# A two-layer hybrid encoder on one core: queries rotated beside their products, the rotary key on 128 partitions at the layer's front, latents left unscaled

## The chip, the core and the metric

The kernel runs on one core of a Trainium2 chip. A core has TensorE (matrix products into PSUM), VectorE, ScalarE and GpSimd for elementwise work, SyncE, which issues most DMA transfers, and DMA engines. Each engine works through its own list of instructions in order; they meet only at semaphores. The metric is the device time of one execution in microseconds (us). Before the change the median of three executions was 1465.46 us (1462.36 to 1467.71).

## The reference

The model is an encoder of two layers over 1024 tokens of width 1024, all in fp32. Per layer, cut to what matters here:

```
u = rmsnorm(h, ln_mix) @ w_in            # split by columns:
c_q, c_kv, k_rope, gate_a, gq, gk, gv, lr_f, lr_b, gate_g = split(u)
# attention (4 heads): latents normed, expanded; a shared rotary key
q = rmsnorm(c_q, q_norm) @ w_uq          # per head 128 plain + 64 rotary columns
k, v = rmsnorm(c_kv, kv_norm) @ w_ukv
scores = q_plain @ k.T + rope(q_rot) @ rope(k_rope).T
y_mla = softmax(scores * scale) @ v * silu(gate_a)
# gated linear attention (4 heads), forward and backward
la = log_sigmoid(lr @ w_g + b_g) / 16    # decay, cumulated in chunks of 64
y_gla = rmsnorm(gla(gq, gk, gv, la)) * silu(gate_g)
h = h + concat(y_mla, y_gla) @ w_out
h = h + sigmoid(rmsnorm(h) @ w_gate) * (p[i] @ w_proj)
```

`rope(x)` splits 64 columns into halves x1, x2 and gives (x1 cos - x2 sin, x1 sin + x2 cos). `rmsnorm(x)` is x / sqrt(mean(x²) + 1e-6), times a gain.

## The kernel before

Everything is kept transposed: 128 features on the partitions, 1024 tokens along the free dimension. To reach fp32 accuracy every operand is split into a high and a low part (names end in h and l), and each product is three matmuls: high·high, low·high, high·low (`mm3`, L165). A tile of the input projection (`in_tile`, L314) is 48 matmuls of 512 columns; its weights come in two halves through `load_split` (L139): a DMA into wr, a ScalarE copy that makes wh (L146), a ScalarE copy with scale -1 that puts -wh into wl (L150) and a GpSimd DMA that adds the weights to it (L151). There are five buffers each of wh and wl, so a split waits until TensorE is through with the block five loads earlier that has the buffer. PSUM has tiles of two banks under two tags, "mm" and "aux", two tiles each.

The input's norm factor r_x (1 / rms per token, as a full tile) is computed by `rstd` (L174): ScalarE makes sqh, VectorE sql, TensorE sums over the partitions (L185), VectorE does a Newton iteration on small tiles (nwa, nwy, nwt). Since the norm is not applied to the projection's input, each evacuation multiplies by r_x.

A layer is a list of steps, written as a string per layer (ORDER, L50). Q, K, V, G: queries, keys, values and gates of the linear attention. Z: decay of one head (z, Exp, Ln, scans on VectorE, d, exponentials). S: chunk states of one head (transposes L420, products L433, ten ScalarE copies, 28 VectorE state steps L460, then the masked products `afb`, L472). O: output of one head and its norm (o, o2, sqh). C and D: the key-value and query latents (`latent_tile`, L507: the VectorE product craw, then Square on ScalarE); N and M: their norms (L514). A: attention gates. X: the two tiles of rotary query columns of all heads (`q_pairs`), which stay in both "aux" tiles of PSUM, and the loads of the cosine and sine tables. E: the rotated key (`rotary_key`, L583), on 32 partitions at a time. T: the rotated queries (`rotary_queries`, L607), whose parts go to the heads' tiles qs by 16 DMAs. H: a head's plain queries (qh, ql). k, v: a head's keys (kh, kll) and values. s: scores, b: attention products, y and w: output projection. A "+" swaps the PSUM tag of a step.

The string gives priorities. A scheduler then sets the order of each engine's list from them and from its own estimate of times, so that a step moved in the string can move others.

Of the kernel before, what the change touches and what calls it, by code (L numbers as in the profile page):

```python
# [19 lines left out]
P = 128  # L20
# [26 lines left out]


WTAG = "aux"
ORDER = ("K0 R0 Q0 G0+ Z0 V0 K1 S0 Z1 V1 O0 S1 Q1 D0 Z2 G1 G2 P0 O1 S2 C0 Z3 D1 C1 N0 D2 O2 S3 G3 M0 A0 O3 X0 A1 E0 A2 A3+ H0 k0 T0 s0 v0 H2 k1+ s1 k2 b0 H1 k3 s2 y1 b1 H3+ s3 b2 v1 s4 y0 y3 b3 y2 s5 b4 w0 w1+ s6 w2 b5 w3+ s7 w4 b6 w5+ s8 w6 w7 b7",  # L50
         "Q0 K0 Z0 V0 S0 Z1 V1 S1 Q1 K1 Z2 G0 O0 S2 G1 Z3 G2+ C0 O1 D0 O2 S3 G3 C1 N0 D1 D2+ O3 M0 X0 A0 A1 E0 A2 k0 y2 H0 A3 T0 s0 v0 H3 k1+ s1 H1 b0 H2 s2 k2 b1 s3 y0 k3+ b2 v1 s4 y3 y1 b3 s5 b4 w0 w1+ s6 w2+ b5 w3 s7 w4 b6 w5+ s8 w6+ w7 b7")

ENG = dict(at="V", qi="V", qb="P", og="P", gate="P", sq="V", kT="A", put="A", o="A", ple="A", hadd="V")
TCKW = {"schedule_with_timeline_sim": True}
# [3 lines left out]
def hybrid_encoder(ctx: ExitStack, tc: tile.TileContext, xT, pT, pos, vecs, w_in, wq, wk, wv,  # L58
# [112 lines left out]
                    nc.tensor.matmul(ps[:, c, :], lhsT=a, rhs=b[:, c * HC:(c + 1) * HC],  # L171
                                     start=(i == 0 and j == 0), stop=(i == n - 1 and j == 2))

    def rstd(acc, width, n=S, tmp=st, res=mt, col=None):  # L174

        if isinstance(acc, tuple):
            mat, parts = ones_r.bitcast(F32), acc
        else:
            mat, parts = ones_r, (tmp(dt=F32R, name="sqh"), tmp(dt=F32R, name="sql"))
            split(parts[0][:, :n], parts[1][:, :n], acc)  # L180
        ps = flat(bank2("aux"))
        for c in range(0, n, HC):
# [39 lines left out]
    h1d = dram([8, P, S], "h1d")  # L222
    cosd = dram([32, S], "cosd")
    sind = dram([32, S], "sind")

    def ple_projection(i):
        ops = []
# [12 lines left out]
        for g in range(4):  # L240
            hi, lo = load_split(w_proj[i, g], HC)
            for c in range(2):
# [49 lines left out]
    for L in range(DEPTH):  # L292
# [213 lines left out]

        def latent_tile(t, s2, tile=mt):  # L507
            ps = in_tile(t)
            o = tile(name="craw")
            nc.vector.tensor_tensor(o, flat(ps), r_x, op=ALU.mult)  # L510
            s2.add(o)
            return o

        def latent_norm(raws, s2, off, width):  # L514
            r = rstd(s2.acc, width)
            res = []
            for j, raw in enumerate(raws):
                nc.vector.scalar_tensor_tensor(raw, raw, gv(off, j), r, op0=ALU.mult, op1=ALU.mult)
# [63 lines left out]

        def rotary_key():  # L583

            cos, sin = xx[2:]
            t1, t2 = mt(name="t1"), mt(name="t2")
            k1, k2 = slice(64, 96), slice(96, 128)
            nc.vector.tensor_tensor(t1[0:32], small[k1], cos[k1], op=ALU.mult)
            nc.vector.tensor_tensor(t2[0:32], small[k2], sin[k2], op=ALU.mult)
            nc.vector.tensor_tensor(t1[32:64], small[k1], sin[k1], op=ALU.mult)  # L590
            nc.vector.tensor_tensor(t2[32:64], small[k2], cos[k2], op=ALU.mult)
            nc.vector.tensor_tensor(t1[0:32], t1[0:32], t2[0:32], op=ALU.subtract)
            nc.vector.tensor_tensor(t1[32:64], t1[32:64], t2[32:64], op=ALU.add)
# [353 lines left out]
```

## Time and profile before

| what | before |
|---|---|
| median of three executions | 1465.46 us |
| the profiled execution | 1466.21 us, span 1464.5 us |
| TensorE busy | 1377.6 us, 94% |
| VectorE, ScalarE, GpSimd busy | 856.5, 721.3, 427.6 us |
| granted TensorE clock, mean | 0.979 of full speed |
| DMA | 163.93 MB, 112 GB/s over the span |

The span is what the profiled execution's trace covers; the rest of its time lies around it. Busy times of VectorE and ScalarE are far from the span, so their sums alone say little: what counts is where TensorE stands idle and which engine's instruction ends that. In a timeline's row the bracket at the end gives the idle time before the instruction and what released it. The first layer runs to about 760 us, the second to the end.

### The profile page before, as it was taken

What the parts mean: (1) busy time and instruction counts of PE and PEld (TensorE: products, weight loads), DVE (VectorE), ACT (ScalarE), POOL (GpSimd) and SP (SyncE); (2) the same over time, 40 slices, a digit from 0 to 9 for tenths busy, and PEclk for the clock granted to TensorE, in tenths of its full rate; (3) what the DMA queues carried; (4) which work ended last, traced back from release to release, by engine and by line L of the source; (5) the groups of instructions that cost most, each with busy time, mean ns of one, the idle gap of its engine ahead of it and who ended that gap; (6) DMA issues with size and microseconds to landing.
All of it is one profiled execution on the core that took longest, in us unless ns stands there. A gap on an engine that the chain in (4) does not pass through costs nothing. (4 is left out here: it accounts for less than half of the span.)

```text
span 1464.5 us, 21076 instructions
## 1 busy us (share of the span) xinstructions
PE 1377.6 (94%) x8400; PEld 1167.1 (80%) x8400; DVE 856.5 (58%) x1196; ACT 721.3 (49%) x1013; POOL 427.6 (29%) x312
## 2 busy tenths in 40 slices
PE   8999899998999999999999999889989999999984
PEld 6799778876778788888889877778767888878984
DVE  2576745788446544464455686667745564455547
ACT  6565475544355443364545555534444453345531
POOL 4321212122346454112432211212145564311210
PEclk9999999999999999999999999999999999999997
DMA  8653545346431223355765343324651213335853
GB/s 288 178 124 76 112 104 170 82 101 145 126 82 43 71 67 94 67 112 152 208 155 121 73 95 79 87 66 96 177 134 47 65 51 80 102 73 112 210 130 123
DMA packets 77793, 163.93 MB, mean 112 GB/s; under 512 B 9536, under 2 KB 17088, under 8 KB 77696
## 3 DMA queue, kind: packets, MB, share of 16 engines
q1 hardware_dynamic: 51200, 116.19, 25.9%
q0 software_dynamic: 26496, 46.41, 18.9%
q8 instruction: 66, 1.08, 0.3%
q14 instruction: 31, 0.25, 0.1%
HBM read 128.74 MB, written 25.43 MB: 105 GB/s over the span
## 5 line engine op out<-in xcount | busy, mean ns | idle before, releaser
L150 ACT ACTIVATE wl<-wr 128x512 fp32r<-128x512 f32 (+2 forms) x176 | 107.4, 610 | 316.8 <-PE ps L171 287.5
L680 POOL TENSOR_SCALAR sc<-sc,sums 128x1024 f32<-128x1024 f32 x64 | 182.1, 2856 | 101.5 <-DVE sums L679 95.3
L151 POOL DMA_DIRECT2D wl<-in_w_in x84 | 72.5, 877 | 353.1 <-ACT wl L150 314.8
L146 ACT ACTIVATE wh<-wr 128x512 fp32r<-128x512 f32 (+2 forms) x184 | 110.8, 603 | 30.3 <-PE ps L171 11.9
L678 ACT ACTIVATE sc<-ps,top 128x1024 f32<-128x1024 f32 x64 | 71.4, 1116 | 72.8 <-DVE top L677 67.8
L677 DVE TENSOR_REDUCE top<-ps 128x1 f32<-128x1024 f32 x64 | 78.3, 1224 | 44.2 <-PE ps L672 44.1
L171 PE MATMUL ps<-xh,wh 128*128 128x512 f32 x288 | 92.3, 400 | 10.1 <-DVE gate L366 4.6
L133 DVE TENSOR_TENSOR el<-ps,eh 128x1024 fp32r<-128x1024 f32 x64 | 78.1, 1220 | 40.4 <-ACT eh L132 40.2
L171 PE MATMUL ps<-x0h,wh 128*128 128x512 f32 x288 | 91.5, 399 | 8.9 <-DVE t L613 5.0
L460 DVE SCALAR_TENSOR_TENSOR s<-s,last 64x128 f32<-64x128 f32 x208 | 77.0, 370 | 36.8 <-ACT s L102 29.8
L171 PE MATMUL ps<-x0h,wl 128*128 128x512 f32 x288 | 91.4, 397 | 0.8 <-DMA wl<-in_w_in 0.8
L171 PE MATMUL ps<-xh,wl 128*128 128x512 f32 x288 | 91.5, 396 | 0.0
L171 PE MATMUL ps<-xl,wh 128*128 128x512 f32 x288 | 90.8, 395 | 0.0
L171 PE MATMUL ps<-x0l,wh 128*128 128x512 f32 x288 | 90.4, 395 | 0.0
L132 ACT ACTIVATE eh<-ps 128x1024 fp32r<-128x1024 f32 x64 | 65.4, 1022 | 38.9 <-PE ps L693 38.9
L171 PE MATMUL ps<-yh,wh 128*128 128x512 f32 x256 | 79.8, 393 | 1.2 <-DVE h L732 0.9
L171 PE MATMUL ps<-yl,wh 128*128 128x512 f32 x256 | 79.5, 391 | 0.0
L171 PE MATMUL ps<-yh,wl 128*128 128x512 f32 x256 | 79.5, 390 | 0.0
L151 POOL DMA_DIRECT2D wl<-in_w_out x32 | 27.9, 873 | 175.0 <-ACT wl L150 174.9
L171 PEld LDWEIGHTS ps<-xh,wh 128*128 128x128 f32 x288 | 54.4, 192 | 22.8 <-DVE gate L366 5.0
L693 PE MATMUL ps<-ident,sc 128*128 128x128 f32 x512 | 66.3, 273 | 6.2 <-DVE ql L130 3.1
L171 PEld LDWEIGHTS ps<-x0h,wh 128*128 128x128 f32 x288 | 54.7, 192 | 21.6 <-DVE t L613 5.7
(257 smaller groups left out, 3569.0 us busy)
## 6 DMA issues: line engine op xcount, KB each, us to landing
wr<-in_w_in SPq DMA_DIRECT2D x88, 256.0 KB, 3.4
wl<-in_w_in POOLq DMA_DIRECT2D x84, 256.0 KB, 4.9
wr<-in_w_gate SPq DMA_DIRECT2D x40, 256.0 KB, 3.2
projd<-po SPq DMA_DIRECT2D x16, 512.0 KB, 4.6
wr<-in_w_out SPq DMA_DIRECT2D x32, 256.0 KB, 3.3
wl<-in_w_out POOLq DMA_DIRECT2D x32, 256.0 KB, 4.7
wl<-in_w_gate POOLq DMA_DIRECT2D x32, 256.0 KB, 4.7
xraw<-in_xT SPq DMA_DIRECT2D x8, 512.0 KB, 5.9
```

The lines of the kernel that those rows point to most:

```text
L132: nc.scalar.activation(hi, src, AF.Copy)
L133: nc.vector.tensor_tensor(lo, src, hi.bitcast(F32), op=ALU.subtract)
L146: nc.scalar.activation(hi[:, :n], raw[:, :n], AF.Copy)
L150: nc.scalar.activation(lo[:, :n], raw[:, :n], AF.Copy, scale=-1.0)
L151: nc.gpsimd.dma_start(lo[:, :n], src, accum_op=ALU.add)
L171: nc.tensor.matmul(ps[:, c, :], lhsT=a, rhs=b[:, c * HC:(c + 1) * HC], start=(i == 0 and j == 0), stop=(i == n - 1 and j == 2))
L460: nc.vector.scalar_tensor_tensor(state(n)[rows], state(m)[rows], alpha[rows, m:m + 1], state(n)[rows], op0=ALU.mult, op1=ALU.add)
L677: nc.vector.tensor_reduce(m, flat(ps), axis=AX.X, op=ALU.max, negate=True)
L678: nc.scalar.activation(e, flat(ps), AF.Exp, bias=m, accum_out=sums[:, b:b + 1])
L680: nc.gpsimd.tensor_scalar(e, e, sums[:, b:b + 1], None, op0=ALU.mult)
L693: nc.tensor.transpose(out=ps[:, j, b * P:(b + 1) * P], in_=e[:, kt], identity=ident)
```

## The change

Three parts. The order strings: E goes from behind A1 (beside X0) to the layer's front, and T goes from behind H0, k0 (first layer) or A3 (second) to right behind X0. The key: `rotary_key` fetches its two halves by eight DMAs into 128 partitions (four token quarters of 32 features), does its products 256 columns wide there, splits once, writes the parts to a DRAM tile krd and loads ks and kl from it; sine and cosine stay in a constant tile sc4 for this. The latents: `latent_tile` copies the PSUM tile unscaled with ScalarE, Square reads PSUM too, and `latent_norm` corrects the epsilon term: since craw lacks the factor r_x, the norm needs EPS times (mean(x²) + EPS) in place of EPS, which `ax` and `base` carry.

```diff
@@ ORDER
-  "K0 R0 Q0 G0+ Z0 V0 ... O3 X0 A1 E0 A2 A3+ H0 k0 T0 s0 v0 ..."
+  "K0 R0 E0 Q0 G0+ Z0 V0 ... O3 X0 T0 A1 A2 A3+ H0 k0 s0 v0 ..."
-  "Q0 K0 Z0 V0 ... X0 A0 A1 E0 A2 k0 y2 H0 A3 T0 s0 v0 ..."
+  "Q0 K0 E0 Z0 V0 ... X0 T0 A0 A1 A2 k0 y2 H0 A3 s0 v0 ..."
@@ rstd
-        nc.vector.tensor_scalar(a, ..., 0.5 / width, 0.5 * EPS,
-                                op0=ALU.mult, op1=ALU.add)
+        nc.vector.tensor_scalar(a, ..., 0.5 / width,
+                                0.0 if base is not None else 0.5 * EPS, op0=ALU.mult, op1=ALU.add)
+        if base is not None:
+            nc.vector.scalar_tensor_tensor(a, base, EPS, a, op0=ALU.mult, op1=ALU.add)
+        if ax is not None:
+            nc.vector.tensor_copy(ax, a)
@@ latent_tile
             o = tile(name="craw")
-            nc.vector.tensor_tensor(o, flat(ps), r_x, op=ALU.mult)
-            s2.add(o)
+            nc.scalar.activation(o, flat(ps), AF.Copy)
+            s2.add(flat(ps))
@@ latent_norm
-            r = rstd(s2.acc, width)
+            r = rstd(s2.acc, width, base=ax)
@@ rotary_key
-            cos, sin = xx[2:]
-            t1, t2 = mt(name="t1"), mt(name="t2")
...
-            nc.scalar.activation(ks[0:64], t1[0:64], AF.Copy)
-            nc.scalar.activation(ks[64:128], t1[0:64], AF.Copy)
-            for half in (slice(0, 64), slice(64, 128)):
-                nc.vector.tensor_tensor(kl[half], t1[0:64], ks[0:64].bitcast(F32), op=ALU.subtract)
+            n = S // 4
+            work = mt(name="kr")
+            k1, k2, u1, u2 = (work[:, i * n:(i + 1) * n] for i in range(4))
+            rot = mt(name="krot")[:, :2 * n]
+            cos, sin = sc4[:, 0], sc4[:, 1]
+            for b in range(4):
+                for k, row in ((k1, 64), (k2, 96)):
+                    nc.sync.dma_start(k[b * 32:(b + 1) * 32], small[row:row + 32, b * n:(b + 1) * n])
+            for x1, x2, o, op in ((cos, sin, rot[:, :n], ALU.subtract), (sin, cos, rot[:, n:], ALU.add)):
+                nc.vector.tensor_tensor(u1, k1, x1, op=ALU.mult)
+                nc.vector.tensor_tensor(u2, k2, x2, op=ALU.mult)
+                nc.vector.tensor_tensor(o, u1, u2, op=op)
+            parts = mt(F32R, "krp").rearrange("p (h c) -> p h c", h=2)
+            split(parts[:, 0], parts[:, 1], rot)
             ks, kl = mt(F32R, "ks"), mt(F32R, "kl")
+            for i, t in enumerate((ks, kl)):
+                for b in range(4):
+                    nc.sync.dma_start(krd[L, i, :, :, b * n:(b + 1) * n].rearrange("j f n -> f j n"),
+                                      parts[b * 32:(b + 1) * 32, i].bitcast(F32).rearrange("p (j n) -> p j n", j=2))
+                for half in (slice(0, 64), slice(64, 128)):
+                    nc.sync.dma_start(t[half].bitcast(F32), krd[L, i].rearrange("j f n -> (j f) n"))
```

Lines of the changed file stand 10 to 20 higher than before: L393 to L396 there are L382 to L385 here (z, a, and its two functions), L633 to L635 are L613 to L615, L377 is L366, L697 is L677, L514 is L503, L210 is L205.

ScalarE at the front of the second layer, before. z_6460 is the bias step of Z0, wl and wh with 6658 belong to V0's fourth weight block, those with 6858, 6913, 6968 and 7023 to V1's four.

```order
L150 ACTIVATE wl_6658<-wr_6656 128x512
L146 ACTIVATE wh_6657<-wr_6656 128x512
L150 ACTIVATE wl_6858<-wr_6856 128x512
L146 ACTIVATE wh_6857<-wr_6856 128x512
L382 ACTIVATE z_6460<-ps_6457,vec_92 128x1024
L383 ACTIVATE a_6461<-ps_6457,vec_92 128x1024
```

The same place of the changed kernel: z_6520 is Z0's bias step, krp_6500 the key's split, 6973, 7028 and 7083 are V1's second to fourth blocks.

```order
L150 ACTIVATE wl_6973<-wr_6971 128x512
L146 ACTIVATE wh_6972<-wr_6971 128x512
L132 ACTIVATE krp_6500<-krot_6485 128x512
L150 ACTIVATE wl_7028<-wr_7026 128x512
L146 ACTIVATE wh_7027<-wr_7026 128x512
L150 ACTIVATE wl_7083<-wr_7081 128x512
L146 ACTIVATE wh_7082<-wr_7081 128x512
L393 ACTIVATE z_6520<-ps_6517,vec_92 128x1024
L394 ACTIVATE a_6521<-ps_6517,vec_92 128x1024
```

Z0's steps moved behind the key's split and the splits of three more weight blocks.

ScalarE at Z1 of the second layer, before (s1_6727 is the last of the ten state copies, 7197 is the second block of Q1).

```order
L102 ACTIVATE s1_6727<-ps_6744 64x128
L382 ACTIVATE z_6825<-ps_6822,vec_92 128x1024
L383 ACTIVATE a_6826<-ps_6822,vec_92 128x1024
L384 ACTIVATE a_6826<-a_6826 128x1024
L385 ACT_TABLE_LOAD
L385 ACTIVATE a_6826<-a_6826 128x1024
L150 ACTIVATE wl_7197<-wr_7195 128x512
```

And in the changed kernel (7319 and 7326 are K1's two blocks).

```order
L102 ACTIVATE s1_6787<-ps_6804 64x128
L150 ACTIVATE wl_7319<-wr_7317 128x512
L146 ACTIVATE wh_7318<-wr_7317 128x512
L393 ACTIVATE z_6885<-ps_6882,vec_92 128x1024
L394 ACTIVATE a_6886<-ps_6882,vec_92 128x1024
L395 ACTIVATE a_6886<-a_6886 128x1024
L150 ACTIVATE wl_7326<-wr_7324 128x512
L146 ACTIVATE wh_7325<-wr_7324 128x512
L396 ACT_TABLE_LOAD
L396 ACTIVATE a_6886<-a_6886 128x1024
```

A weight block's split now stands between Z1's Exp and its Ln.

VectorE at the rotated queries of the first layer, before (ps_3082 and ps_3108 are X0's two tiles in PSUM, gate_3348 the gate of A3).

```order
L130 SCALAR_TENSOR_TENSOR ql_3379<-ps_3359,qh_3378 128x1024
L503 SCALAR_TENSOR_TENSOR o_3041<-o_3041,vec_92,rstd_3054 128x1024
L133 TENSOR_TENSOR kll_3403<-ps_3389,kh_3402 128x1024
L613 TENSOR_TENSOR t1_3406<-ps_3082,cos_3127 128x1024
L614 TENSOR_TENSOR t2_3407<-ps_3108,sin_3128 128x1024
L615 TENSOR_TENSOR t1_3406<-t1_3406,t2_3407 128x1024
L130 SCALAR_TENSOR_TENSOR rl_3412<-t1_3406,rh_3411 128x1024
L613 TENSOR_TENSOR t1_3415<-ps_3082,sin_3128 128x1024
L614 TENSOR_TENSOR t2_3416<-ps_3108,cos_3127 128x1024
L615 TENSOR_TENSOR t1_3415<-t1_3415,t2_3416 128x1024
L130 SCALAR_TENSOR_TENSOR rl_3421<-t1_3415,rh_3420 128x1024
L366 TENSOR_TENSOR gate_3348<-ps_3285,rstd_351 128x1024
```

And in the changed kernel (ps_3121 and ps_3147 are X0's tiles; ahead of the first row here stand t1_3176 from ps_3121 and the gate of A2).

```order
L210 STREAM_TRANSPOSE rstd_3093<-nwy_3096 128x1024
L634 TENSOR_TENSOR t2_3177<-ps_3147,sin_3167 128x1024
L514 SCALAR_TENSOR_TENSOR o_3080<-o_3080,vec_92,rstd_3093 128x1024
L635 TENSOR_TENSOR t1_3176<-t1_3176,t2_3177 128x1024
L130 SCALAR_TENSOR_TENSOR rl_3182<-t1_3176,rh_3181 128x1024
L633 TENSOR_TENSOR t1_3185<-ps_3121,sin_3167 128x1024
L634 TENSOR_TENSOR t2_3186<-ps_3147,cos_3166 128x1024
L635 TENSOR_TENSOR t1_3185<-t1_3185,t2_3186 128x1024
L130 SCALAR_TENSOR_TENSOR rl_3191<-t1_3185,rh_3190 128x1024
L377 TENSOR_TENSOR gate_3411<-ps_3348,rstd_354 128x1024
L130 SCALAR_TENSOR_TENSOR ql_3442<-ps_3422,qh_3441 128x1024
L133 TENSOR_TENSOR kll_3466<-ps_3452,kh_3465 128x1024
```

The queries' rotation moved ahead of ql and kll, and the gate of A3 with it.

## Rows read from the trace of the kernel before

**Rows 1.** The page: busy us of an engine, share, instructions

```profile
PE 1377.6 (94%) x8400; PEld 1167.1 (80%) x8400; DVE 856.5 (58%) x1196; ACT 721.3 (49%) x1013; POOL 427.6 (29%) x312
```

**Rows 2.** Timeline of TensorE, first layer: start us, us, instruction, [idle before]

```profile
350.20 0.61 PE L171 MATMUL ps<-ch,wh 128*128 128x512 f32 x2
...
369.63 1.22 PE L171 MATMUL ps<-x0h,wh 128*128 128x512 f32 x2 [4.99 <-DVE t L613]
...
374.75 0.62 PE L171 MATMUL ps<-x0l,wh 128*128 128x512 f32 x2
...
382.00 0.39 PE L672 MATMUL ps<-kh,qh 128*128 128x512 f32 x1
```

**Rows 3.** Windows: start:end us, length, busy times, granted clock, DMA

```profile
370.00:383.00 13.00, 13.00 (x53) 10.58 (x53) 3.96 (x4) 2.87 (x5) 1.30 (x2) 0.90 0.66 149
```

**Rows 4.** Timeline of VectorE, first layer, around the rotations

```profile
345.54 1.21 DVE L588 TENSOR_TENSOR t<-small,cos 32x1024 f32<-32x1024 f32 x1 [2.98 <-DMA cos<-cosd]
...
357.84 1.25 DVE L205 STREAM_TRANSPOSE rstd<-nwy 128x1024 f32<-128x1024 f32 x1
...
367.22 1.23 DVE L130 SCALAR_TENSOR_TENSOR rl<-t,rh 128x1024 fp32r<-128x1024 f32 x1 [1.18 <-ACT rh L129]
...
369.50 1.22 DVE L614 TENSOR_TENSOR t<-ps,cos 128x1024 f32<-128x1024 f32 x1
```

**Rows 5.** Timeline of TensorE, second layer, first rotary scores

```profile
1071.93 0.77 PE L672 MATMUL ps<-ks,qs 128*128 128x512 f32 x1 [5.51 <-DMA qs<-rl]
```

**Rows 6.** Timeline of VectorE, second layer, first and last operation of T0

```profile
1054.88 1.22 DVE L613 TENSOR_TENSOR t<-ps,cos 128x1024 f32<-128x1024 f32 x1
...
1067.22 1.22 DVE L130 SCALAR_TENSOR_TENSOR rl<-t,rh 128x1024 fp32r<-128x1024 f32 x1 [1.12 <-ACT rh L129]
```

**Rows 7.** Timeline of ScalarE, front of the second layer

```profile
777.19 1.12 ACT L382 ACTIVATE z<-ps,vec 128x1024 f32<-128x1024 f32 x1
...
781.71 1.28 ACT L385 ACT_TABLE_LOAD   x1
...
783.00 1.06 ACT L385 ACTIVATE a<-a 128x1024 f32<-128x1024 f32 x1
...
784.26 0.63 ACT L150 ACTIVATE wl<-wr 128x512 fp32r<-128x512 f32 x1 [0.19 <-PE ps L352]
...
784.79 0.62 ACT L146 ACTIVATE wh<-wr 128x512 fp32r<-128x512 f32 x1
```

**Rows 8.** Timeline of VectorE, front of the second layer

```profile
784.10 1.23 DVE L386 SCALAR_TENSOR_TENSOR z<-z,a 128x1024 f32<-128x1024 f32 x1 [5.13 <-ACT a L385]
...
790.57 1.23 DVE L397 TENSOR_TENSOR d<-b,ref 128x1024 f32<-128x1024 f32 x1
...
798.80 2.41 DVE L358 TENSOR_TENSOR gv<-ps,rc 128x1024 f32<-128x1024 f32 x2
...
809.90 3.00 DVE L460 SCALAR_TENSOR_TENSOR s<-s,last 64x128 f32<-64x128 f32 x8
...
814.35 1.27 DVE L472 COPY_PREDICATED afb<-mask,ps 128x1024 f32<-128x1024 uint32 x1
```

**Rows 9.** Timeline of TensorE, front of the second layer

```profile
776.52 0.63 PE L378 MATMUL ps<-lr,wzt 96*128 96x512 f32 x2
...
799.78 1.04 PE L420 MATMUL ps<-ident,gqk 128*128 128x128 f32 x8
...
860.61 0.72 PE L171 MATMUL ps<-xh,wh 128*128 128x512 f32 x2 [1.80 <-DVE gqk L337]
...
881.77 0.50 PE L185 MATMUL ps<-sqh,ones_r 128*128 128x512 f32 x1 [0.45 <-ACT sqh L132]
```

**Rows 10.** Groups by line: busy us, mean ns | idle before, releaser

```profile
L510 DVE TENSOR_TENSOR craw<-ps,rstd 128x1024 f32<-128x1024 f32 x10 | 12.1, 1219 | 0.1
...
L501 ACT ACTIVATE o<-ps 128x1024 f32<-128x1024 f32 x8 | 8.1, 1019 | 0.0
...
L102 ACT ACTIVATE o<-ps 128x1024 f32<-128x1024 f32 x8 | 8.1, 1013 | 0.8 <-PE ps L492 0.8
```

More of the change, by code (lines that the diff above doesn't have):

```diff
@@ L49 @@
 WTAG = "aux"
-ORDER = ("K0 R0 Q0 G0+ Z0 V0 K1 S0 Z1 V1 O0 S1 Q1 D0 Z2 G1 G2 P0 O1 S2 C0 Z3 D1 C1 N0 D2 O2 S3 G3 M0 A0 O3 X0 A1 E0 A2 A3+ H0 k0 T0 s0 v0 H2 k1+ s1 k2 b0 H1 k3 s2 y1 b1 H3+ s3 b2 v1 s4 y0 y3 b3 y2 s5 b4 w0 w1+ s6 w2 b5 w3+ s7 w4 b6 w5+ s8 w6 w7 b7",
-         "Q0 K0 Z0 V0 S0 Z1 V1 S1 Q1 K1 Z2 G0 O0 S2 G1 Z3 G2+ C0 O1 D0 O2 S3 G3 C1 N0 D1 D2+ O3 M0 X0 A0 A1 E0 A2 k0 y2 H0 A3 T0 s0 v0 H3 k1+ s1 H1 b0 H2 s2 k2 b1 s3 y0 k3+ b2 v1 s4 y3 y1 b3 s5 b4 w0 w1+ s6 w2+ b5 w3 s7 w4 b6 w5+ s8 w6+ w7 b7")
+ORDER = ("K0 R0 E0 Q0 G0+ Z0 V0 K1 S0 Z1 V1 O0 S1 Q1 D0 Z2 G1 G2 P0 O1 S2 C0 Z3 D1 C1 N0 D2 O2 S3 G3 M0 A0 O3 X0 T0 A1 A2 A3+ H0 k0 s0 v0 H2 k1+ s1 k2 b0 H1 k3 s2 y1 b1 H3+ s3 b2 v1 s4 y0 y3 b3 y2 s5 b4 w0 w1+ s6 w2 b5 w3+ s7 w4 b6 w5+ s8 w6 w7 b7",
+         "Q0 K0 E0 Z0 V0 S0 Z1 V1 S1 Q1 K1 Z2 G0 O0 S2 G1 Z3 G2+ C0 O1 D0 O2 S3 G3 C1 N0 D1 D2+ O3 M0 X0 T0 A0 A1 A2 k0 y2 H0 A3 s0 v0 H3 k1+ s1 H1 b0 H2 s2 k2 b1 s3 y0 k3+ b2 v1 s4 y3 y1 b3 s5 b4 w0 w1+ s6 w2+ b5 w3 s7 w4 b6 w5+ s8 w6+ w7 b7")
 ENG = dict(at="V", qi="V", qb="P", og="P", gate="P", sq="V", kT="A", put="A", o="A", ple="A", hadd="V")
@@ L172, in mm3, with rstd @@
                                      start=(i == 0 and j == 0), stop=(i == n - 1 and j == 2))
-    def rstd(acc, width, n=S, tmp=st, res=mt, col=None):
+    def rstd(acc, width, n=S, tmp=st, res=mt, col=None, ax=None, base=None):
         if isinstance(acc, tuple):
@@ L191, in rstd @@
         t = cp.tile([P, 32], F32, tag="nwt", name="nwt", bufs=2)[:, :nb]
-        nc.vector.tensor_scalar(a, r[:, :n].rearrange("p (b i) -> p b i", i=32)[:, :, 0], 0.5 / width, 0.5 * EPS,
-                                op0=ALU.mult, op1=ALU.add)
+        nc.vector.tensor_scalar(a, r[:, :n].rearrange("p (b i) -> p b i", i=32)[:, :, 0], 0.5 / width,
+                                0.0 if base is not None else 0.5 * EPS, op0=ALU.mult, op1=ALU.add)
[3 more added lines that the diff above has]
+            nc.vector.tensor_copy(ax, a)
         nc.vector.tensor_scalar(y.bitcast(I32), a.bitcast(I32), 1, None, op0=ALU.arith_shift_right)
@@ L224, in hybrid_encoder @@
     sind = dram([32, S], "sind")
+    krd = dram([DEPTH, 2, 2, 32, S], "krd")
     def ple_projection(i):
@@ L248, in ple_projection @@
                 nc.sync.dma_start(projd[i][g * 2 + c], o)
+    sc4 = cp.tile([P, 2, S // 4], F32, name="sc4")
     def rotary_tables():
@@ L254, in rotary_tables @@
         work = mt(name="rot")
-        kk, ang, *rs = (work[:, i * n:(i + 1) * n] for i in range(4))
+        kk, ang = (work[:, i * n:(i + 1) * n] for i in range(2))
+        rs = sc4[:, 1], sc4[:, 0]
         posi = kk.bitcast(I32)
@@ L302, in hybrid_encoder @@
         rc = cp.tile([P, 8], F32, tag="rc", name="rc", bufs=2)
-        r_x = rstd(sq.acc, D, col=rc)
+        ax = cp.tile([P, 32], F32, tag="ax", name="ax", bufs=2)
+        r_x = rstd(sq.acc, D, col=rc, ax=ax)
         afb = mt(name="afb").rearrange("p (d t c) -> p d t c", d=2, c=CH)
@@ L583, in rotary_key @@
         def rotary_key():
-            cos, sin = xx[2:]
-            t1, t2 = mt(name="t1"), mt(name="t2")
[L587 to L593, printed above, removed]
-            ks, kl = mt(F32R, "ks"), mt(F32R, "kl")
-            nc.scalar.activation(ks[0:64], t1[0:64], AF.Copy)
-            nc.scalar.activation(ks[64:128], t1[0:64], AF.Copy)
-            for half in (slice(0, 64), slice(64, 128)):
-                nc.vector.tensor_tensor(kl[half], t1[0:64], ks[0:64].bitcast(F32), op=ALU.subtract)
+            n = S // 4
[12 more added lines that the diff above has]
+            split(parts[:, 0], parts[:, 1], rot)
+            ks, kl = mt(F32R, "ks"), mt(F32R, "kl")
+            for i, t in enumerate((ks, kl)):
[4 more added lines that the diff above has]
+                    nc.sync.dma_start(t[half].bitcast(F32), krd[L, i].rearrange("j f n -> (j f) n"))
             ksl.extend((ks, kl))
```

## The prediction, written before the changed kernel ran

> **What bounds the kernel.** I read the busy shares first: TensorE is busy for 94% of the span [rows 1], so the kernel is as long as TensorE's work plus its waits. A change pays only where it takes away a wait of TensorE, and costs only where it adds one. Next I read TensorE's timeline around the places that the edits touch, then the timelines of VectorE and ScalarE beside it, to see which wait ends last. The reader is to see two stretches that lose much, and one, the front of the second layer, that loses little now.
>
> In the first layer the lost stretch runs from the first matmul of H0 at 350.20 to the first full score at 382.00 [rows 2]: 31.8 us. It holds 18 + 12 + 48 matmuls of H0, k0 and A3 and 6 of scores. The last 32 of A3 took 7.25 us (374.75 to 382.00), 0.227 each, so 84 should take 19.1 us: 12.7 are lost. One piece is named in the row at 369.63: A3 waited 4.99 us for VectorE's L614 product, because A3 goes into a PSUM bank that the rotated queries (X0) still held. After that wait the clock fell: the first 16 matmuls took 5.12 us (369.63 to 374.75) instead of 3.63, so a wait of this size costs 1.5 us more, at the lower level of 1.2 GHz; the mean grant from 370 to 383 was 0.90 [rows 3]. In the second layer the scores waited 5.51 us for the transfers into qs [rows 5].
>
> **The change part by part.**
>
> *Queries rotated beside X0, first layer.* Today VectorE does the key's six products (from 345.54) before anything of the queries, and frees the banks when the second L614 ends at 370.72 [rows 4]. Now the key is gone from here. From 345.6 VectorE does seven operations of 1.22 (three L613/L614 products ahead of the freeing one, it, the sum, rl and a gate), a transpose of 1.25, an output product about as long, 1.1 of small ones, and waits 1.2 for ScalarE's rh [rows 4]: 13.3, so the banks are free at 358.9. TensorE is through with k0 at 358.0 and loses 0.9. A3 then ends near 369.7, and VectorE's queue holds the gate of A3, ql and kll in that order: 3.7 us until kll, which the scores need. Loss 4.6 in place of 12.7: **-8.1 us**. Ends: -11 if the scores' first products hide most of the 3.7; -4 if the cosine table lands later, as it already held VectorE for 2.98 us.
>
> *The same, second layer.* VectorE works on T0 from 1054.88 to 1068.44, 13.6 us [rows 6]; TensorE gets its data 3.5 us after that [rows 5]. X0 ends near 1038.1, so the queries now land near 1055.2; the scores can use them from 1066.4, where the wait begins. The 5.51 goes with its 1.5 of clock; kll starts about 0.5 later: **-6.5 us** (-4 to -8).
>
> *Key at the front.* It removes eight VectorE operations of 1.21 to 1.22 per layer from the place above (counted there) and adds seven short ones, one ScalarE copy and 20 transfers at the front. Nobody needs ks and kl until the scores, hundreds of us later, so the transfers are hidden. In the first layer the Z0 chain comes about 4 us later but S0 has more slack than that: **+0.5** (0 to 2). In the second layer the instruction order changes, and this is where I think the loss is. Steps, in times of the profile before:
>
> 1. The bias step z of Z0 runs at 777.19 now, right behind its matmuls at 776.52 [rows 7, 9]. It now stands on ScalarE behind the split of the third and fourth weight blocks of V1 (wl_7028, wl_7083). There are five wl buffers; wl_7083's is free only when TensorE has finished the third of V0's four blocks. V0 runs from about 776.4 to 799.78, so that is 794.0; with one wl and wh (1.15, [rows 7]) z starts at 795.2, 18.0 late.
> 2. From z to the end of L397's d it is 14.6 us (777.19 to 791.80) [rows 7, 8], now to 809.8; V0's evacuation gv, 1.2 each, is queued behind it: 811.2. TensorE meanwhile does V1's first half (96 of V0's 192 matmuls took 11.5) to 811.3 and Q1's first half (24 of 0.227) to 816.8: nothing lost yet. S0's transposes stood 8.0 after d (799.78), with about 1 to spare, and gv takes some of that: 817.2.
> 3. From transposes to the end of afb it was 15.8 (799.78 to 815.62) [rows 8, 9]. Now 2.4 of matmuls between go, and five more state steps (0.375 each, [rows 8]) stand before afb: 15.2, so 832.4. V1's second half goes into that bank; TensorE is there at 828.8. Lost 3.6, and 1.5 of clock.
> 4. Z1's Ln stands behind a wl whose buffer needs V1's first block of the second half. From there wl/wh 1.15, table 1.28, Ln 1.06, then 7.7 to d and 1.4 to gv, whose bank K1 needs: K1 starts 4.0 after V1 ends (847.7 without the clock), again with 1.5 of clock.
> 5. From K1 the chain transposes, copies, 13 state steps, afb and two gqk ends at 871.6, where G0 starts. Before: 860.61 [rows 9]. TensorE is 11 us late there.
> 6. VectorE now works S1's left-over state steps in between Z2's scans, so Z2's d ends at 884.8. ScalarE then has table, exponentials, loads, the gate's Silu (behind d's product and the gate on VectorE), o, o2, sqh: 15.4 us, to 900.2. TensorE stands at 891.9 and waits 8.3 for sqh. Before it waited 0.45 there, at 881.77 [rows 9]: **18.4 late**.
>
> To this come the clock of steps 3 and 4 (two times 1.5, both on the chain) and half of it at step 6 (0.7), and one latent copy that ScalarE now does ahead of the next sqh (1.0): **+23.1 us**. Ends: +11, if only the delay seen at G0 stays; +28, if every new wait costs its full clock and the later waits grow. I take 23 since every step follows from instructions that stand one behind the other.
>
> *Latents.* Ten VectorE products of 1.22 [rows 10] go, ten ScalarE copies of about 1.01 come (o is the same kind of copy, 1.013), and Square reads PSUM (o2: 1.019). Where VectorE stood on the path it gives some tenths, where ScalarE is queued it takes 1.0; one of these is counted above, the rest I put at **0** (-2 to +4). The Trainium skill, page "ScalarE: Activation LUTs", section "Rules for kernel authors", says to keep multiplications on VectorE rather than ScalarE. The rows speak against it here, in fp32 out of PSUM: 1.01 against 1.22. By the rule the ten moves could only lose; that is rival 3.
>
> Sum: 0.5 - 8.1 - 6.5 + 23.1 + 0 = +9.0. The profiled execution took 1466.21 (span 1464.5), 0.75 above the median of 1465.46; so 1475.2 against it, and **1474.5** as a median.
>
> **Rivals.**
>
> *1. The front costs half, and the parts cancel.* If the wait at step 6 is filled because VectorE takes the state steps faster than I laid them out, G0's 11 us with its clock remain, some 14: 0.5 - 8.1 - 6.5 + 14 = 0, so 1465. For it: steps 5 and 6 are sums of twenty small terms, in each of which I could be 0.3 off. Against: 18 us of late start at step 1 have to go somewhere, and TensorE has only V1's and Q1's halves to fill them.
>
> *2. Faster: the late start is covered.* V1's first half and Q1's first half are 17 us of work that TensorE does not need Z0 for, and the late start is 18. If the evacuations then keep up (what decides is whether TensorE finds the bank of V1's second half free at 828.8), the front costs 1 to 3 and the two freed waits remain: 0.5 - 8.1 - 6.5 + 2 = -12, so 1453. For it: up to step 2 my own count shows no loss. Against: afb ends 15 us after S0's transposes today, and nothing in the change shortens that.
>
> *3. Slower still: ScalarE becomes the queue.* Each of ten latent tiles now holds its bank for two ScalarE operations in a row, and weight splits stand behind them on ScalarE. If all ten delays of 1.0 end on TensorE, 9 more us: 1483.5. For it: TensorE already waits for sqh, behind ScalarE's queue, at 881.77 [rows 9]. Against: the copies replace a VectorE step that Square had to wait for.
>
> *4. The key's trip through memory fails to hide* would show as a wait of scores for ks; no chance of its own, since 270 us lie between.
>
> **How the numbers follow.** What can be told from no change is about 0.3%, 4.4 us. The forecast has a chance of 0.50, rival 1 0.23, rival 2 0.17, rival 3 0.10. Slower by over 0.3%: forecast and rival 3, 0.60. Within: rival 1, 0.23. Faster: rival 2, 0.17. The forecast's own range is 1469 to 1481. The range of eight in ten goes from 1458, which takes in rival 1 and the upper part of rival 2, to 1485, which takes in rival 3.
>
> **What would show it.** Right: in the second layer z of Z0 near 795 instead of 777, counted from the same start of V0; gv behind it; new waits of TensorE on afb at V1's second half, on gv at K1 and on sqh at O0, of about 3.6, 4.0 and 8; no wait for qs in the second layer; A3 of the first layer starting within 2 us after k0. Wrong: G0 of the second layer starting less than 5 us later after V0's start than before (84.2 us); a wait of 3 us or more left before A3 of the first layer; scores waiting for ks, kl or qs.

## The result and the profile after

The changed kernel takes 1483.84 us (median of four executions, 1481.65 to 1484.56) against 1463.91 us beside it. The ratio is 1.0125, 95% interval 1.0112 to 1.0139. It is slower, as forecast, but by 18 to 20 us where the sum said 9: outside the forecast's own range (1469 to 1481), inside the range of eight in ten (to 1485). The profiled execution took 1483.96 us with a span of 1482.3.

The page's row of busy times, as [rows 1]:

```profile
PE 1383.9 (93%) x8400; PEld 1173.8 (79%) x8400; DVE 836.9 (56%) x1190; ACT 724.5 (49%) x1019; POOL 428.9 (29%) x312
```

TensorE executes the same 8400 matmuls; they took 6.3 us longer, so 11.5 of the 17.8 us of span are idle time. The other 6.3 go with a lower granted clock, 0.973 in the mean where it was 0.979. VectorE got 20 us less to do and the kernel still grew.

**Front of the second layer, after.** First ScalarE, then VectorE, then TensorE, the same stretch as [rows 7], [rows 8] and [rows 9]. Everything stands 3.0 us earlier than before, since the matmuls of Z0 run at 773.54 where they ran at 776.52.

```profile
786.28 0.62 ACT L150 ACTIVATE wl<-wr 128x512 fp32r<-128x512 f32 x1
...
791.12 0.63 ACT L150 ACTIVATE wl<-wr 128x512 fp32r<-128x512 f32 x1 [3.69 <-PE ps L363]
791.65 0.62 ACT L146 ACTIVATE wh<-wr 128x512 fp32r<-128x512 f32 x1
792.18 1.10 ACT L393 ACTIVATE z<-ps,vec 128x1024 f32<-128x1024 f32 x1
```

```profile
805.53 1.23 DVE L408 TENSOR_TENSOR d<-b,ref 128x1024 f32<-128x1024 f32 x1
...
807.00 2.36 DVE L369 TENSOR_TENSOR gv<-ps,rc 128x1024 f32<-128x1024 f32 x2
...
829.46 1.29 DVE L483 COPY_PREDICATED afb<-mask,ps 128x1024 f32<-128x1024 uint32 x1
```

```profile
773.54 0.63 PE L389 MATMUL ps<-lr,wzt 96*128 96x512 f32 x2
...
814.82 1.09 PE L431 MATMUL ps<-ident,gqk 128*128 128x128 f32 x8 [0.75 <-DVE gqk L419]
...
830.81 0.58 PE L363 MATMUL ps<-wh,xh 128*128 128x256 f32 x1 [4.48 <-DVE afb L483]
...
847.86 1.19 PE L171 MATMUL ps<-xh,wh 128*128 128x512 f32 x2 [4.02 <-DVE gv L369]
...
869.63 3.68 PE L497 MATMUL ps<-b,s 128*64 128x64 f32 x64 [2.29 <-DVE afb L483]
...
873.66 1.16 PE L171 MATMUL ps<-xh,wh 128*128 128x512 f32 x2
...
901.14 0.79 PE L186 MATMUL ps<-sqh,ones_r 128*128 128x512 f32 x1 [6.41 <-ACT sqh L132]
...
993.18 1.22 PE L171 MATMUL ps<-xh,wh 128*128 128x512 f32 x2 [4.57 <-DVE gate L377]
```

The bias step z runs 18.6 us after its matmuls; before it was 0.7 (776.52 to 777.19). The split at 791.12 is what it stood behind: that split waited 3.69 us for TensorE to leave a weight buffer. The three new waits of TensorE follow: 4.48 on afb, 4.02 on gv, 6.41 on sqh.

What such waits cost in clock shows in the windows behind the one on afb (830.81), the one on sqh (901.14) and the one on a gate (993.18). In a windows row the third number from the end is the granted clock, and the two behind it are DMA's share and GB/s.

```profile
830.00:835.00 5.00, 4.19 (x24) 4.19 (x25) 1.80 (x3) 0.15 (x1) 0.00 (x0) 0.66 0.00 0
...
901.00:906.00 5.00, 4.86 (x17) 4.06 (x18) 2.84 (x4) 2.16 (x4) 1.28 (x3) 0.57 0.25 65
993.00:998.00 5.00, 4.82 (x12) 3.84 (x13) 1.35 (x2) 3.91 (x5) 0.00 (x0) 0.55 0.07 24
```

The means of 0.55 to 0.66 show that behind each wait the matmuls ran at the lower level, 1.2 GHz, for most of these 5 us. The wait on a gate is not new: the kernel before has one of 4.60 at 973.34.

**Around the rotated queries, after.** First layer, TensorE, VectorE and ScalarE, beside [rows 2] and [rows 4]:

```profile
348.08 0.62 PE L171 MATMUL ps<-ch,wh 128*128 128x512 f32 x2
...
359.37 1.22 PE L171 MATMUL ps<-x0h,wh 128*128 128x512 f32 x2 [4.33 <-DVE t L633]
...
362.81 0.62 PE L171 MATMUL ps<-x0h,wl 128*128 128x512 f32 x2
...
376.28 1.22 PE L692 MATMUL ps<-kh,qh 128*128 128x512 f32 x2 [4.23 <-ACT kh L132]
...
379.79 0.40 PE L692 MATMUL ps<-kl,qs 128*128 128x512 f32 x1
...
404.54 1.09 PE L713 MATMUL ps<-ident,sc 128*128 128x128 f32 x8 [1.56 <-DVE ql L130]
```

```profile
346.94 1.23 DVE L633 TENSOR_TENSOR t<-ps,cos 128x1024 f32<-128x1024 f32 x1 [3.33 <-DMA cos<-cosd]
...
356.00 2.17 DVE L130 SCALAR_TENSOR_TENSOR rl<-t,rh 128x1024 fp32r<-128x1024 f32 x1 [1.12 <-ACT rh L129]
358.10 1.21 DVE L633 TENSOR_TENSOR t<-ps,sin 128x1024 f32<-128x1024 f32 x1
...
372.08 1.23 DVE L377 TENSOR_TENSOR gate<-ps,rstd 128x1024 f32<-128x1024 f32 x1 [8.03 <-PE ps L171]
```

```profile
371.63 0.53 ACT L150 ACTIVATE wl<-wr 128x384 fp32r<-128x384 f32 x1 [4.57 <-DMA qs<-rh]
...
373.34 1.06 ACT L378 ACTIVATE gate<-gate 128x1024 f32<-128x1024 f32 x1 [0.74 <-DVE gate L377]
374.31 1.01 ACT L129 ACTIVATE qh<-ps 128x1024 fp32r<-128x1024 f32 x1
375.21 1.02 ACT L132 ACTIVATE kh<-ps 128x1024 fp32r<-128x1024 f32 x1
```

H0 and k0 were through on TensorE at 355.03, but their copies qh and kh ran on ScalarE at 374.31 and 375.21, behind a weight split and behind the gate of A3. The reader is to see the chain: A3 needs a bank that VectorE's rotation holds, the gate needs A3, kh stands behind the gate, and the first scores need kh. In the kernel before, the same stretch had, beside the wait of 4.99 in [rows 2], these two on TensorE:

```profile
360.44 0.50 PE L672 MATMUL ps<-kh,qh 128*128 128x512 f32 x1 [2.42 <-ACT kh L132]
...
362.57 0.80 PE L672 MATMUL ps<-kll,qh 128*128 128x512 f32 x1 [1.40 <-DVE kll L133]
```

So 8.8 us of waits became 8.6: in this place TensorE waits as long as before. In the second layer, TensorE after, beside [rows 5]:

```profile
1068.32 0.70 PE L171 MATMUL ps<-ch,wh 128*128 128x512 f32 x2 [1.39 <-DVE gate L377]
...
1075.42 0.75 PE L171 MATMUL ps<-xh,wh 128*128 128x512 f32 x2 [2.74 <-DVE kll L133]
...
1114.58 1.09 PE L713 MATMUL ps<-ident,sc 128*128 128x128 f32 x8 [1.56 <-DVE ql L130]
```

The wait for qs (5.51) is gone; 1.39 and 2.74 stand in its place, and before there was one of 1.76 on kll.

### The profile page after: what moved, and what is told of

Its sections match the earlier page's. It is cut to its first block, busy times and chain, and to the rows that moved or that the text cites. A ratio compares the mean times of both kernels' runs of the same rounds, so it can differ in the third digit from the quotient of the medians.

```text
span 1482.3 us, 21156 instructions
## 1 busy us (share of the span) xinstructions
PE 1383.9 (93%) x8400; PEld 1173.8 (79%) x8400; DVE 836.9 (56%) x1190; ACT 724.5 (49%) x1019; POOL 428.9 (29%) x312
## 3 DMA queue, kind: packets, MB, share of 16 engines
q8 instruction: 66, 1.08, 0.3%
## 5 line engine op out<-in xcount | busy, mean ns | idle before, releaser
L697 DVE TENSOR_REDUCE top<-ps 128x1 f32<-128x1024 f32 x64 | 78.3, 1224 | 42.0 <-PE ps L692 41.8
L713 PEld LDWEIGHTS ps<-ident,sc 128*128 128x128 f32 x512 | 59.4, 141 | 14.8 <-DVE ql L130 3.6
```

The costliest lines, as they stand in the source:

```text
L697: nc.vector.tensor_reduce(m, flat(ps), axis=AX.X, op=ALU.max, negate=True)
L713: nc.tensor.transpose(out=ps[:, j, b * P:(b + 1) * P], in_=e[:, kt], identity=ident)
```

## The experiments

The first four shared runs of the kernel before (1465.48), the next four others (1466.03), the last one its own (1467.40). Ratios are to the kernel before.

### The key behind Z0

Only the second layer's string differs from the changed kernel.

```diff
-  "Q0 K0 E0 Z0 V0 ...
+  "Q0 K0 Z0 E0 V0 ...
```

> The changed kernel with one edit: in the second layer's string the key's step E0 stands behind Z0 instead of ahead of it. The key is still built at the front, on 128 partitions, with its 20 transfers. Theory: the loss comes from Z0's bias step standing on ScalarE behind the splits of V1's weight blocks, and E0 ahead of Z0 is what put it there. Then the time falls from 1483.8 to about 1462 (1459 to 1465), z follows its matmuls at once, and TensorE's waits on afb (4.5), gv (4.0) and sqh (6.4) at that front shrink to those of before. Rival (the key's transfers, or the ten ScalarE copies of the latents, load the queues): most of the loss stays, above 1478.

Measured: 1462.72, ratio 0.9987 (0.9974 to 1.0000). TensorE's Z0 and ScalarE's z in its trace:

```profile
770.37 0.63 PE L389 MATMUL ps<-lr,wzt 96*128 96x512 f32 x2
```

```profile
771.03 1.12 ACT L393 ACTIVATE z<-ps,vec 128x1024 f32<-128x1024 f32 x1
```

z is 0.66 behind its matmuls again, and the kernel is 21.1 us faster than the changed one; from the kernel before it can hardly be told. From Z0's matmuls to the gate wait it is now 201.5 us (that wait ends at 971.82); in the changed kernel it is 219.6, before 196.8. So of the 22.1 us between the two spans 18.2 lie in this stretch. Another 3.2 lie ahead of it, where the string is the same: 1.5 of them before 48 us, where a weight transfer landed later; the rest isn't explained. All the operations of the key are still there, behind Z0. The stretch is still 4.6 longer than before; the other 18.2 were their place in the order. Not every wait shrank to that of before, as had been expected: TensorE still waits 4.91 on afb (at 853.82, before 1.42 at 857.23) and 2.28 on sqh (at 880.59, before 0.45). What makes these was not tested.

### The early rotation alone

The kernel before, with T moved and nothing else.

```diff
-  ... X0 A1 E0 A2 A3+ H0 k0 T0 s0 ...      ... X0 A0 A1 E0 A2 k0 y2 H0 A3 T0 s0 ...
+  ... X0 T0 A1 E0 A2 A3+ H0 k0 s0 ...      ... X0 T0 A0 A1 E0 A2 k0 y2 H0 A3 s0 ...
```

> The kernel before with only the queries' rotation moved: T0 right behind X0 in both strings, the key still on 32 partitions beside X0. VectorE's order then has the key's six products of 1.22 behind the queries and, in the first layer, behind the gate of A3, ahead of ql and kll. Theory (the early rotation pays only when the key's VectorE work is gone from there and kh is not late on ScalarE): the wait for qs in the second layer goes (-5 to -7), but kll of the first layer comes about 7 later: 1460 to 1470 in all, no gain of the size forecast. Rival (the prediction's size: both waits go): 1450 to 1453.

Measured: 1475.44, ratio 1.0064 (1.0049 to 1.0079). Neither side had expected a loss of this size. TensorE and VectorE in the first layer:

```profile
383.56 1.22 PE L672 MATMUL ps<-kh,qh 128*128 128x512 f32 x2 [12.88 <-ACT kh L132]
```

```profile
371.98 1.22 DVE L588 TENSOR_TENSOR t<-small,cos 32x1024 f32<-32x1024 f32 x1
...
380.51 2.45 DVE L598 TENSOR_TENSOR kl<-t,ks 64x1024 fp32r<-64x1024 f32 x2 [1.12 <-ACT ks L595]
```

The key's eight operations, 1.22 each, did not go away: they now ran behind the rotation, and the key's split on ScalarE stood ahead of qh and kh (kh at 382.49). The scores waited 12.88. The second layer shows the same, 14.02 on kll. So the first two parts of the change belong together: with the key's operations left in that place, the rotation ahead of them made the kernel slower.

### The latents alone

The kernel before, with `latent_tile`, `latent_norm` and `rstd` of the changed kernel.

```diff
-            nc.vector.tensor_tensor(o, flat(ps), r_x, op=ALU.mult)
-            s2.add(o)
+            nc.scalar.activation(o, flat(ps), AF.Copy)
+            s2.add(flat(ps))
```

> The kernel before with only the latents changed (ScalarE copies, Square from PSUM, epsilon corrected in the norm). Theory: ten VectorE products of 1.22 for ten ScalarE copies of 1.0, of which one or two stand on a path: 1462 to 1467. Rival (ScalarE becomes the queue): 1470 to 1475.

Measured: 1466.34, ratio 1.0010 (0.9998 to 1.0023): no difference. Rival 3 falls. In this run's trace the copies took what the prediction took from their neighbour in [rows 10]:

```profile
L515 ACT ACTIVATE craw<-ps 128x1024 f32<-128x1024 f32 x10 | 10.1, 1009 | 0.0
```

### H0 and k0 ahead of the gates

The kernel with the key behind Z0, with the heads moved so that qh and kh don't stand behind A3's gate.

```diff
-  ... X0 T0 A1 A2 A3+ H0 k0 s0 ...      ... X0 T0 A0 A1 A2 k0 y2 H0 A3 s0 ...
+  ... X0 T0 A1 H0 k0 A2 A3+ s0 ...      ... X0 A0 A1 A2 k0 T0 y2 H0 A3 s0 ...
```

> As the first kernel of this call, and in addition other orders around X0: first layer X0 T0 A1 H0 k0 A2 A3+, so that ScalarE copies qh and kh ahead of the gates and weight splits of A2 and A3; second layer X0 A0 A1 A2 k0 T0 y2 H0 A3, so that kh and kll come ahead of the rotated queries. Theory: the forecast gain of the early rotation was eaten by kh, which stood on ScalarE behind work that waited for A3 (4.2 us of TensorE's wait in the first layer) and behind rh (2.7 in the second). Then this is 4 to 9 below the first kernel: 1453 to 1458. Rival (the gain is lost to VectorE's own queue or to the tables' transfer): within 2 of the first kernel.

Measured: 1473.11, ratio 1.0045 (1.0028 to 1.0061). The theory, that ScalarE's queue alone had eaten the gain, fell. The wait for kh is gone, and TensorE has this instead:

```profile
360.20 1.19 PE L171 MATMUL ps<-x0h,wh 128*128 128x512 f32 x2 [11.23 <-DVE t L633]
```

A3 follows sooner in TensorE's order and needs the bank that the rotation holds until 360.1, whatever ScalarE does. There are two limits one behind the other, and taking away the second makes TensorE wait at the first. That wait is 3.1 longer than the two that it replaces. Another 4.6 of new waits stand ahead of it (2.66 on a state step, 0.79 and 1.12 on a latent and its norm, at 325.88 to 344.59), since the edit moved other steps too. In the second layer 4.26 on qh replaced 1.39 and 2.74, and that stretch kept its length. The run showed what to try next: TensorE needs work there that is in neither chain.

### The rotation without its tables

The kernel with the key behind Z0; in the first layer the rotation multiplies by r_x in place of cosine and sine, and the tables aren't loaded, so the queries there are not rotated: it serves for its time alone.

```diff
+            if L == 0:
+                xx.extend((r_x, r_x))
+                return
             cs = mt(name="cos"), mt(name="sin")
```

> The kernel with the key behind Z0 (1462.7), but in the first layer the queries' rotation multiplies by the norm factor r_x, which lies ready, in place of the cosine and sine tables, and the eight loads of the tables are left out there. Left out: the right rotation of the first layer's queries. Every engine's order of compute work stays. Theory (in the first layer the early rotation is bound by when VectorE can begin it, and it waits 2.90 us for the cosine table): L633 begins about 2.9 earlier, TensorE's wait of 3.91 before A3 falls to about 1, the wait for kh before the scores stays near 4 since it follows A3's end through VectorE's gate and ScalarE; time 1459 to 1460. Rival (the end of the rotation is set by the key query's norm and the splits queued between its operations, not by its beginning): A3 still waits 3 or more and the time stays within 1 us of 1462.7.

Measured: 1459.86, ratio 0.9960 (0.9947 to 0.9974), 2.9 less than the kernel that it was made from (measured beside other runs of the kernel before). VectorE begins at 342.39 in place of 345.12, and TensorE shows these waits:

```profile
355.11 0.73 PE L171 MATMUL ps<-x0h,wh 128*128 128x512 f32 x2 [1.42 <-DVE t L636]
...
370.51 1.22 PE L695 MATMUL ps<-kh,qh 128*128 128x512 f32 x2 [4.23 <-ACT kh L132]
```

The wait before A3 fell from 3.91 to 1.42, the one on kh stayed at 4.23 to the hundredth. So the cosine table's landing makes 2.5 of the 3.9 us before A3, and the kh wait follows A3 at a fixed distance. In this trace 3.3 us are gained at the wait on el (411.37 for 414.68) and 0.8 are left at the gate wait of the second layer (971.04 for 971.82): between two profiled executions a few us can move in places that no edit touched, so the local rows decide here and not the spans.

### Three orders that give TensorE other work

All three are the kernel with the key behind Z0. v0 (a head's values) goes ahead of the scores, and A3 and the heads change banks ("+").

```diff
 kernel with the key behind Z0
   ... X0 T0 A1 A2 A3+ H0 k0 s0 v0 H2 ...       ... X0 T0 A0 A1 A2 k0 y2 H0 A3 s0 v0 H3 ...
 first
+  ... X0 T0 A1 A2 A3 H0+ k0+ v0 s0 H2 ...      ... X0 T0 A0 A1 A2 A3 H0+ k0+ v0 y2 s0 H3 ...
 second
+  ... X0 T0 A1 A2 A3 H0+ k0+ s0 v0 H2 ...      ... X0 A0 A1 A2 k0 H0 T0 y2 A3 s0 v0 H3 ...
 third
+  ... X0 T0 A1 A2 H0 A3 k0+ v0 s0 H2 ...       ... X0 T0 A0 A1 k0 H0 A2 y2 A3 s0 v0 H3 ...
```

> The kernel with the key behind Z0 (1462.7), with A3 in the mm banks ahead of H0 and k0 (which go to the aux banks behind the rotation) and v0 ahead of the first scores, in both layers. Theory (two waits follow one another in the first layer: the banks that T0 holds, 3.9, and behind them qh and kh on ScalarE, 4.2; each costs because TensorE has nothing else in its order at that point): A3's 38 last matmuls and part of v0 cover the first to 3 or less, the rest of v0 covers the second to under 1; the first layer gains 4 to 6, the second 2 to 4; time 1453 to 1458. Rival (each engine's queue is full there, so that a filled wait comes back at the next evacuation): the sum of TensorE's waits from X0 to the first scores stays above 7 in the first layer and the time within 2 us of 1462.7.

Measured: 1456.37, ratio 0.9940 (0.9920 to 0.9960). In the second layer TensorE no longer waits between X0 and the first scores. In the first it waits 2.93, 1.66 and 0.53, in all 5.1 for 8.1, and the longest is now for a weight block of v0 that arrives late. Up to the wait on el the first layer gained 3.3 us (411.33 for 414.68), where 4 to 6 had been expected; the second gained 4.7, where it was 2 to 4.

```profile
360.28 0.58 PE L671 MATMUL ps<-wl,ch 128*128 128x256 f32 x1 [2.93 <-DMA wl<-in_wv]
...
376.07 0.50 PE L692 MATMUL ps<-kh,qh 128*128 128x512 f32 x1 [1.66 <-ACT kh L132]
```

> As the kernel before it, but scores ahead of v0 in the first layer, and in the second the rotation behind H0 and k0, so that kh, kll, qh and ql stand ahead of it on ScalarE and VectorE. Theory: in the first layer the wait before H0 is as in the run before, and the wait for kh or kll before the scores is back at 3 to 5; in the second no wait for kll, but the scores or A3 wait for the rotation's end (the banks or qs) by 3 to 6; time 1457 to 1462. Rival (v0 covers nothing, the queues do): first layer as in the run before, within 1 us.

Measured: 1458.70, ratio 0.9957 (0.9937 to 0.9978). First layer: 2.60 before H0 and 2.50 on kh, the same 5.1 in all as with v0 ahead of the scores. The rival was right there: v0 covered nothing, since it waited for its own weights, and what both runs share there is the change of banks, with which A3 runs ahead of H0. Second layer: a wait for qs of 5.55, as in [rows 5].

> The kernel with the key behind Z0 (1462.7), with H0 (first layer) and H0 and k0 (second layer) ahead of the gate A3, so that kh and qh stand right behind the second rh on ScalarE, and v0 ahead of the scores in the first layer. Theory (ScalarE's queue ahead of qh and kh, weight splits and the gate's Silu, is what made the scores late): no wait for kh or kll of more than 2 us in either layer; a wait of 3 to 5 before k0 in the first layer, for the banks that the rotation holds; time 1455 to 1459. Rival (the wait goes over to the gate's tiles A2 and A3, whose banks then come free later): waits on a gate product of 3 or more in the second layer and the time within 2 us of 1462.7.

Measured: 1458.46, ratio 0.9954 (0.9936 to 0.9972). The first layer is the best of all: waits of 1.53 (on a gate) and 0.55, and none for the rotation's banks, where 3 to 5 had been expected, because H0, A3 and then k0 fill the time until the rotation has left them. It reached the wait on el 9.0 us sooner than the kernel with the key behind Z0 (405.63 for 414.68). The second layer is bad, in a way that neither side named:

```profile
1038.48 1.22 PE L692 MATMUL ps<-kh,qh 128*128 128x512 f32 x2 [10.67 <-ACT qh L129]
```

qh stands behind both rh here, which wait for VectorE's rotation.

### The best of both

> The kernel with the key behind Z0 (1462.7), with the first layer's order of the kernel with the heads first and the second layer's order of the kernel that fills with v0. Counted on TensorE from the last common wait ahead of each place: the first layer's order gained 9.0 us up to the first layer's wait for el, the second layer's 4.7 up to the second's. Theory (the two places are independent): 1462.7 - 9.0 - 4.7 = 1449, 1447 to 1452. Rival (part of a gain made in the first layer is given back at a later wait, as in the run with the heads first, whose second layer is not comparable): 1453 to 1457.

Measured: 1446.80 (1445.10 to 1450.04), ratio 0.9866 (0.9846 to 0.9886), 2 us better than the sum of the two gains (1449) and just under the range expected (1447 to 1452). It beats both kernels. TensorE's waits from 318 to 420, in the first layer (us in total, times, longest us):

```profile
PE ps L713 <- DVE ql L130: 2.2, 1, 2.2
PE ps L171 <- DVE el L133: 1.7, 1, 1.7
PE ps L671 <- DVE gate L377: 0.7, 1, 0.7
PE ps L692 <- ACT kh L132: 0.6, 1, 0.6
```

Neither the rotation's banks nor a late kh hold TensorE now. This kernel keeps all three parts of the change; no run had these orders without them, so what the parts themselves give at their best place isn't separated from what the order gives.

## Why the prediction was right, and where it was wrong

**The front of the second layer: right, in size too.** From Z0's matmuls to the gate wait at 993.18 the changed kernel lost 22.8 us; 23.1 had been worked out. Step by step, with the 3.0 us that the layer starts earlier added to the trace's times: z 795.2 (forecast 795.2), the end of d 809.7 (809.8), transposes 817.8 (817.2), the end of afb 833.7 (832.4), G0 876.6 (871.6, and 874.6 with the 3.0 of clock that were counted apart), O0's sums 22.4 late (18.4, and 21.4 with the clock). The waits were 4.5, 4.0 and 6.4 for 3.6, 4.0 and 8.3. The working was most off at G0, 2.0 late: it let G0 follow the chain's last gqk, but 64 products for O stand ahead of G0, and they waited 2.29 on afb (869.63). The sqh wait behind it was smaller by nearly as much, so that the close total owes something to luck. The first experiment shows that the order makes 18.2 of it, and the key's own work no more than the other 4.6.

**The rotation in the first layer (-8.1): the step that failed.** The front of the first layer cost 0.6 (one wait on po ends at 214.05, before at 213.44), as forecast (0.5). At the wait on ql the layer is 2.75 ahead (404.54, before 407.29), so 3.4 us were gained between the two and not 8.1. The 4.7 that lack go, but for 0.4, to three steps of the working:

- The slow matmuls behind a wait were put at nothing. The first eight of A3 took 3.44 us (359.37 to 362.81) and the first eight scores 3.51 (376.28 to 379.79), where eight at 0.227 take 1.82: 3.3 us in all. The prediction charged the old wait 1.5 for just this, and did not charge the waits that it left.
- The scores started 4.23 behind A3 and not 3.7: 0.5. The prediction had "VectorE's queue holds the gate of A3, ql and kll in that order" and followed that queue alone; ScalarE's copies qh and kh stand behind A3's gate there.
- A3 started at 359.37 and not at 358.9: 0.5. That this came out near was luck: VectorE began 1.3 later than taken (346.94, the table), one rl took 0.94 more, while the bank that A3 needs is the one that L633 reads, free one product earlier than counted. [rows 2] names L613, the same product, at 369.63; the prediction read it as L614.

TensorE was through with k0 at 355.03 and not at 358.0, and so the 0.9 before A3 became 4.33. The prediction's mark for a wrong step, a wait of 3 us or more there, was met. That the table's landing makes the larger part of this wait was shown by leaving it out; that ScalarE's order and the banks form the rest, by the orders that turn or fill it.

Not even the 3.4 are shown to be the rotation's. Two waits of TensorE ahead of it, before:

```profile
279.71 0.50 PE L185 MATMUL ps<-sqh,ones_r 128*128 128x512 f32 x1 [0.98 <-ACT sqh L132]
...
315.84 0.73 PE L171 MATMUL ps<-x0h,wh 128*128 128x512 f32 x2 [2.17 <-DVE gate L366]
```

And after:

```profile
312.26 0.51 PE L186 MATMUL ps<-sqh,ones_r 128*128 128x512 f32 x1 [0.85 <-ACT s L102]
...
313.74 0.73 PE L171 MATMUL ps<-x0h,wh 128*128 128x512 f32 x2 [0.28 <-DVE gate L377]
```

From the wait on po to the one on a gate TensorE does 715 matmuls in both kernels, in 102.4 us before and 99.7 after. These 2.7 us stood in no term; the run with the latents alone has the second pair of waits and 0.7 of the gain, and what gave the rest was not separated. In the rotation's own place, from H0's first matmul on, 86 matmuls took 32.3 us before (from 350.20) and 31.7 after (348.08 to 379.79). So what the rotation gave lies between 0.5 and 3.4, since TensorE came to A3 earlier and waited the longer for its bank.

**The rotation in the second layer (-6.5): mis-sized.** It gave 2.9 (19.8 us late at 993.18, before 973.34; 17.0 at 1114.58, before 1097.60). The wait for qs went as said. "kll starts about 0.5 later" was wrong: kh stood on ScalarE behind the second rh and a weight split that waits for TensorE, and TensorE waited 2.74 on kll and 1.39 on a gate's bank.

**Latents (0): right**, by the run of that part alone. The rule of the Trainium skill weighed there (page "ScalarE: Activation LUTs", section "Rules for kernel authors") puts a multiplication on VectorE and not on ScalarE, with a factor given for bf16; carried over to the ten moves, it would have had them lose. They don't bear it out: in fp32 out of PSUM a move took 1.01 us for 1.22, and the time did not change.

**The sum.** 0.6 - 3.4 (2.7 of it ahead of H0) - 0.2 (until the second layer's start) + 22.8 - 2.9 + 0.8 (behind the scores), within rounding the 17.8 that is the difference of the spans. Of the 8.8 us that the forecast lacked, 8.3 are the two rotations, even with all of the 3.4 put down to the first. Rivals 1 and 2 took the front for 14 or 2, and it was 22.8; rival 3 came nearest to the time and had the wrong reason.

## What to carry to other kernels

When a step is moved forward in a list of priorities, look first at what now stands behind a wait that it does not need: a bias step of 1 us behind a weight split, whose buffer was busy, cost some 20 us, and swapping two steps gave it back. When a wait is removed, follow every engine's queue to the consumer, and not only the one that did the waiting: here the next limits were an evacuation on ScalarE and, ahead of it, a PSUM bank. Charge the waits that stay for the clock as you charge the one that goes. Putting the step that waits further ahead did not beat two limits in a row; an order that gives TensorE other work at that place did, and with the swap it turned 1.3% slower into 1.3% faster.

## What the runs showed of the hardware

One VectorE operation, rl in the first layer, took 2.17 us where its kind takes 1.23. GpSimd's product stood beside it:

```profile
353.83 3.26 POOL L515 TENSOR_TENSOR o<-o,gate 128x1024 f32<-128x1024 f32 x1 [1.67 <-DVE o L514]
```

It ends at 357.09, and rl at 358.17, 1.08 later; the product itself took 3.26 where the same one takes 2.35 in the kernel before, and its start lies beside L635 (353.66 to 354.88) on VectorE. Each looks as if it had waited for the other to finish. The Trainium skill, page "SBUF — State Buffer", section "SBUF: two separate sides", says that VectorE, with two SBUF inputs, and a GpSimd instruction that reads SBUF hold a shared port pair by turns, each for its whole instruction. These rows agree: 354.88 + 2.35 is 357.23, and 357.09 + 1.23 is 358.32. So do the other traces. Of the 44 operations rl in all eleven, 40 took 1.22 or 1.23, with no such product beside them; the four with one beside them, all the first rl of the first layer, took 2.17, 2.18, 2.17 and 1.34, and those products 3.25 to 3.32. Where another order let the product end first, as in the three that give TensorE other work, the same rl took 1.23.
